# When the accumulators of a finished pass are emptied: at once, or one entry later

## The chip, the cores and the metric

The kernel runs on one core of one Trainium2 chip. The metric is the time of one execution on the device in microseconds (us), as the median of several runs. The chip's engines work beside each other, each through its own queue in order: TensorE (PE in the profile) multiplies matrices and sums into PSUM, VectorE (DVE) and ScalarE (ACT) do elementwise work, GpSimd (POOL) and SyncE (SP) do little here beyond starting DMA transfers.

## The reference

One layer of a hybrid decoder trunk over 512 tokens of width 2048, in float32:

```python
h = _rms_norm(x, norm_g[i])
proj = jnp.einsum("bld,dn->bln", h, w_in[i])
(z_ssd, xbc, dt, u_pool, z_pool, q, k, v, z_attn, gate_logits) = jnp.split(proj, IN_SPLITS, axis=-1)
...
gates = jax.nn.sigmoid(gate_logits.reshape(b, seq, N_BRANCHES, D_MODEL))
```

Three branches (a state-space scan, a causal pooling, a dilated attention) follow, are weighted by `gates`, summed and projected. What matters here is a part of `proj`: the columns for q, k, v and z_attn (five blocks of 1024 columns) and those for the gates (six blocks of 1024 columns).

## The kernel before

Each float32 operand is split in two parts, `hi` and `lo`, and a product is three matmuls: hi with hi, hi with lo, lo with hi. For weights that are streamed in, `split` does this: ScalarE casts to `hi` (L153), VectorE subtracts to get `lo` (L156). Both have three buffers, so a cast must wait until the entry three before has been multiplied. Between the two, L155 lets VectorE make the operand sum of the entry behind it (`mix`) if there is one. `split(idx + 2)` runs two entries ahead of the one that is multiplied.

The eleven blocks are computed by `s_block` with seven products in place of eight, in the manner of Strassen and Winograd: sums of the weight quarters a, b, c, d (T1, T2, T3, T4) are multiplied with sums of the quarters of h (S1 to S4, made once) or with the quarters themselves (L11, L12, L22). A block has three passes over four steps `e` of the contraction: L11, S2, S3 in the first, S4 and S1 in the second, L12 and L22 in the third; L12 goes on in L11's accumulators. One product at one step is an *entry*: 12 matmuls of 128x128 by 128x512 (L364), four steps each, 28 entries a block. Each product has two accumulators of one PSUM bank each, for the two halves of its rows, called `pg`; in this phase there are six such banks (`set_banks(2)`).

When a product is complete (e is 3), `after` empties its accumulators: L11 is copied by ScalarE (L330), the others are added by VectorE into `st` tiles in SBUF (L332, L335, L337, L340, L341, L347). At the end of S1 and of L22 two results of 512 columns each are complete, and L12 gives another; `evac` sends them out: in the gate blocks ScalarE takes a sigmoid (L566) and starts the store (L568) on its own DMA queue, in the q/k/v blocks it copies where needed (L574) and starts the store (L576). The order of work on each engine is the order in which the program is written; nothing is rescheduled. SP loads the weights, issued by `load` inside `split`.

So on VectorE and ScalarE there stand, entry by entry, the split for two entries ahead, and at the end of a pass the emptying of the accumulators, which needs TensorE to be done with that entry.

Of the kernel before, what the change touches and what calls it, by code (L numbers as in the profile page):

```python
# [31 lines left out]
def hybrid_kernel(ctx: ExitStack, tc: tile.TileContext, x, p, norm_g, w_in, conv_w, conv_b, dt_bias, a_log,  # L32
# [17 lines left out]
    def swap(name, as_=None):  # L50
        held["stack"].close()
        held["stack"] = ctx.enter_context(ExitStack())
        if name == "tp":
            held["tp"] = held["stack"].enter_context(tc.tile_pool(name="tq", bufs=NT))
        else:
            held["sp"] = held["stack"].enter_context(tc.tile_pool(name="sp", bufs=1))
# [9 lines left out]
    def set_banks(n):  # L66

        if banks:
            banks["stack"].close()
        banks["n"] = n  # L70
        banks["stack"] = ctx.enter_context(ExitStack())
        banks["psum"] = banks["stack"].enter_context(tc.tile_pool(name=f"psum{len(plan)}", bufs=3, space=PSUM))
# [4 lines left out]
    def PG():  # L77
        return banks["psum"].tile([128, L], F32, name="pg", tag="g", bufs=8 - banks["n"])
# [18 lines left out]
    def tick():  # L97
        now["t"] += 1
        step(other)
        step(tasks)  # L100
        step(third)
# [30 lines left out]
    def split(n):  # L132
        while state["split"] <= n and state["split"] < len(plan):
            i = state["split"]
            if callable(plan[i]) and "sp" not in held:
                return
            load(i)
            if callable(plan[i]):
                plan[i]("mix")
                r, k, c = plan[i]("raw"), 2, L  # L140
            else:
                r = raws.pop(i)
                _, k, c = plan[i]
            if c == 32:

                hl = wp.tile([128, k, 2 * c], F32R, name="hi", tag="hi")
                A.copy(hl[:, :, 0:c], r)
                V.tensor_sub(hl[:, :, c:], r, hl[:, :, 0:c].bitcast(F32))
                parts[i] = hl
            else:  # L150
                hi = wp.tile([128, k, c], F32R, name="hi", tag="hi")
                lo = wp.tile([128, k, c], F32R, name="lo", tag="lo")
                A.copy(hi, r)  # L153
                if state["dma"] > i + 1 and callable(plan[i + 1]):
                    plan[i + 1]("mix")  # L155
                V.tensor_tensor(lo, r, hi.bitcast(F32), op=ALU.subtract)  # L156
                parts[i] = (hi, lo)
            if callable(plan[i]):
                plan[i]("done")
            state["split"] += 1  # L160
            load(i + 3)
# [63 lines left out]
    def hook(f):  # L225
        jobs.append((f, lambda: None))
# [10 lines left out]
    def left(name, kt, t):  # L237
        c = slice(128 * t, 128 * t + 128)
        if name[0] == "L":
            q = slice(256 * (name[1] == "2") + 128 * t, 256 * (name[1] == "2") + 128 * t + 128)  # L240
            kt += 8 * (name[2] == "2")
            return HT[0][:, kt, q], HT[1][:, kt, q]
        return SC[name][0][:, kt, c], SC[name][1][:, kt, c]

    def make_left():
# [8 lines left out]
        for q0 in (0, 4):  # L254
# [13 lines left out]
            for n, o in (("S2", "L11"), ("S3", "S3"), ("S4", "L12"), ("S1", "L22")):  # L268
# [3 lines left out]
                if n in ("S3", "S1"):  # L272
                    yield

    def s_block(c0, evac):
        raw, ps, st = {}, {}, {}

        def src(n, e):
            r = e * 256 + (1024 if n in "cd" else 0)
            c = c0 + (L if n in "bd" else 0)  # L280
            return w_in[r:r + 256, c:c + L].rearrange("(k p) c -> p k c", p=128)

        def fetch(n, e, small):
            if small:
                t = held["sp"].tile([128, 2, L], F32, name="rs", tag="rs", bufs=2)
            else:
                t = wp.tile([128, 2, L], F32, name="raw", tag="raw", bufs=3)
            nc.sync.dma_start(out=t, in_=src(n, e))
            raw[n, e] = t

        def entry(name, e, loads):
            mixed = []

            def f(what):
                if what == "load":
                    for n, small in loads:
                        fetch(n, e, small)
                elif what == "mix":
                    if mixed:
                        return  # L300
                    mixed.append(1)
                    if name == "T2":
                        V.tensor_sub(raw["b", e], raw["d", e], raw["b", e])
                        t = held["sp"].tile([128, 2, L], F32, name="t2", tag="t2", bufs=4)
                        V.tensor_add(t, raw["b", e], raw["a", e])
                        raw["T2", e] = t
                    elif name == "T1":
                        t = held["sp"].tile([128, 2, L], F32, name="t1", tag="rs", bufs=2)
                        V.tensor_sub(t, raw["d", e], raw["T2", e])
                        raw["T1", e] = t  # L310
                    elif name == "T4":
                        V.tensor_sub(raw["T2", e], raw["T2", e], raw["c", e])
                elif what == "raw":
                    return raw[{"T3": "b", "T4": "T2"}.get(name, name), e]
            plan.append(f)
            return len(plan) - 1

        passes = []
        passes.append([(entry("a", e, (("a", False),)), entry("T2", e, (("b", True), ("d", False))),
                        entry("T3", e, ())) for e in range(4)])  # L320
        passes.append([(entry("d", e, (("d", False),)), entry("T1", e, ())) for e in range(4)])
        passes.append([(entry("c", e, (("c", False),)), entry("T4", e, ())) for e in range(4)])
        lefts = (("L11", "S2", "S3"), ("S4", "S1"), ("L12", "L22"))

        def after(name):
            for t in range(2):
                p = ps[name][t]
                if name == "L11":
                    st["u2", t] = st_tile()
                    A.copy(st["u2", t], p)  # L330
                elif name == "S2":
                    V.tensor_add(st["u2", t], st["u2", t], p)  # L332
                elif name == "S3":
                    st["u3", t] = st_tile()
                    V.tensor_add(st["u3", t], st["u2", t], p)  # L335
                elif name == "S4":
                    V.tensor_add(st["u2", t], st["u2", t], p)  # L337
                elif name == "S1":
                    o = st_tile()
                    V.tensor_add(st["u2", t], st["u2", t], p)  # L340
                    V.tensor_add(o, st["u3", t], p)  # L341
                    evac(t, 1, st["u2", t], st["u2", t])
                    evac(2 + t, 1, o, o)
                elif name == "L12":
                    evac(t, 0, p, st_tile())
                elif name == "L22":
                    V.tensor_sub(st["u3", t], st["u3", t], p)  # L347
                    evac(2 + t, 0, st["u3", t], st["u3", t])

        def run():  # L350
            for es, names in zip(passes, lefts):
                for e in range(4):
                    for idx, name in zip(es[e], names):
                        split(idx + 2)
                        hi, lo = parts.pop(idx)
                        if e == 0:
                            ps[name] = ps.pop("L11") if name == "L12" else [PG(), PG()]
                        for t in range(2):
                            for k in range(2):
                                kt = 2 * e + k  # L360
                                xh, xl = left(name, kt, t)
                                first, last = e == 0 and k == 0 and name != "L12", e == 3 and k == 1
                                for i, (lh, r) in enumerate(((xh, hi), (xh, lo), (xl, hi))):
                                    PE.matmul(ps[name][t], lhsT=lh, rhs=r[:, k], start=first and i == 0,  # L364
                                              stop=last and i == 2, skip_group_check=name in ("L11", "L12"))
                        if e == 3:
                            after(name)
                        tick()
        jobs.append((None, run))


# [59 lines left out]
    def st_tile():  # L431
        return held["sp"].tile([128, L], F32, name="st", tag="st", bufs=8)
# [195 lines left out]
    for br in (2, 0, 1):  # L628
        for j in (0, 2):
            s_block(GATES + br * D + j * L, gate_evac(br, j))  # L630
    hook(lambda: (swap("tp"), set_banks(3)))


    qT, kT, vv, oo, stat = {}, {}, {}, {}, {}
# [744 lines left out]
```

## Time and profile before

| | us |
|---|---|
| median of 3 runs | 2635.47 |
| lowest, highest | 2631.3, 2638.95 |
| the profiled execution | 2636.33 |
| its span, first to last instruction | 2634.5 |
| TensorE busy | 2594.7 (98%) |
| VectorE busy | 1545.5 (59%) |
| ScalarE busy | 1004.3 (38%) |

The seven-product phase runs from 151 to about 1009 us of the span, the five q/k/v blocks first (to 588 us), then the six gate blocks. A matmul's row shows its start and a modelled length; matmuls overlap, so lost time is read from the distance of two starts. "Granted clock" is the share of TensorE's full clock: 1.00 or 0.50.

### The profile page before, as it was taken

Reading aid. Unit: us, or ns where it says so; the run is one execution under the profiler, and the core shown is the slowest. Engines: PE = TensorE matmul, PEld = TensorE weight load, DVE = VectorE, ACT = ScalarE, POOL = GpSimd, SP = SyncE. Lnnn points to the kernel's source line nnn. Section 1 sums busy time; section 2 is a strip of 40 time slices with the busy share of each in tenths; the row PEclk is TensorE's granted clock in tenths of the full one; section 3 lists DMA queues with packets and bytes.
Section 4 is the critical chain, followed back from the end, with each engine's and each line's share of the span. In section 5 each row is a group of like instructions: output and inputs, shape, how many; then the busy total and the mean of one; then the engine's idle time right before and its main releaser. Section 6 shows DMA issues by size and latency. Waiting matters only on the chain.

```text
span 2634.5 us, 30399 instructions
## 1 busy us (share of the span) xinstructions
PE 2594.7 (98%) x11924; PEld 2136.4 (81%) x11924; DVE 1545.5 (59%) x1926; ACT 1004.3 (38%) x1275; POOL 190.9 (7%) x213
## 2 busy tenths in 40 slices
PE   9999999999999999999999999999999999999998
PEld 7778888887778787888888888877888888788887
DVE  5767777777777774454536567786642433233333
ACT  5434444444444443343434544543321322232322
POOL 2000000000000000101010001231011111000000
PEclk9999999999999999999999999999999999999999
DMA  6445555455554454434343444463543633333442
GB/s 226 117 136 176 176 164 160 149 160 168 171 173 145 148 155 139 125 104 144 113 140 120 132 125 139 124 186 113 153 147 113 211 107 125 104 121 112 130 142 96
DMA packets 237647, 374.52 MB, mean 142 GB/s; under 512 B 17208, under 2 KB 102020, under 8 KB 236992
## 3 DMA queue, kind: packets, MB, share of 16 engines
q1 hardware_dynamic: 218384, 331.31, 42.0%
q10 hardware_dynamic: 13904, 25.30, 2.6%
q0 software_dynamic: 5216, 15.98, 1.6%
q8 instruction: 93, 1.52, 0.2%
q14 instruction: 50, 0.41, 0.0%
HBM read 330.30 MB, written 42.23 MB: 141 GB/s over the span
## 4 chain that ended last, share of the span: by engine, by line
PE 90%; DVE 4%; ACT 3%; issue 1%; ACTq 1%; DMA 1%; POOL 0%; SPq 0%; DVEq 0%
PE pg L364 28%; PE pg L166 19%; PE pg L167 19%; PE pg L168 19%; ACT hi L153 1%; DVE lo L156 1%; ACT st L566 1%; PE ps L518 1%; PE ps L1079 1%; ACTq L568 1%; PE ps L797 0%; PE ps L761 0%; PE ps L1062 0%; DVE bc L1032 0%; PE ps L716 0%
## 5 line engine op out<-in xcount | busy, mean ns | idle before, releaser
L156 DVE TENSOR_TENSOR lo<-raw,hi 128x1024 fp32r<-128x1024 f32 x424 | 523.0, 1234 | 636.8 <-ACT hi L153 635.0
L153 ACT CAST hi<-raw 128x1024 fp32r<-128x1024 f32 x424 | 444.7, 1051 | 792.3 <-PE pg L168 440.1
L166 PE MATMUL pg<-hh,hi 128*128 128x512 f32 x1152 | 460.7, 400 | 2.0 <-ACT st L566 2.0
L168 PE MATMUL pg<-hh,lo 128*128 128x512 f32 x1152 | 449.6, 390 | 0.0
L167 PE MATMUL pg<-hl,hi 128*128 128x512 f32 x1152 | 449.2, 390 | 0.0
L166 PEld LDWEIGHTS pg<-hh,hi 128*128 128x128 f32 x1152 | 216.8, 188 | 49.9 <-issue 3.3
L168 PEld LDWEIGHTS pg<-hh,lo 128*128 128x128 f32 x1152 | 216.5, 188 | 46.0
L167 PEld LDWEIGHTS pg<-hl,hi 128*128 128x128 f32 x1152 | 216.8, 188 | 45.2 <-issue 2.4
L156 DVE TENSOR_TENSOR lo<-t,hi 128x1024 fp32r<-128x1024 f32 x132 | 161.6, 1224 | 105.8 <-ACT hi L153 105.3
L153 ACT CAST hi<-t 128x1024 fp32r<-128x1024 f32 x132 | 138.8, 1052 | 204.5 <-PE pg L364 168.1
L364 PE MATMUL pg<-lo,hh 128*128 128x512 f32 x528 | 208.3, 394 | 7.0 <-DVE lo L156 7.0
L364 PE MATMUL pg<-hi,hh 128*128 128x512 f32 x528 | 208.0, 394 | 7.0 <-DVE st L612 4.8
L364 PE MATMUL pg<-hi,hl 128*128 128x512 f32 x528 | 206.8, 392 | 0.0
L364 PEld LDWEIGHTS pg<-lo,hh 128*128 128x128 f32 x528 | 100.1, 190 | 32.1 <-DVE lo L156 11.0
L364 PEld LDWEIGHTS pg<-hi,hh 128*128 128x128 f32 x528 | 99.9, 189 | 30.8 <-issue 5.2
L364 PEld LDWEIGHTS pg<-hi,hl 128*128 128x128 f32 x528 | 100.1, 190 | 20.6
L166 PE MATMUL pg<-hi,mh 128*128 128x512 f32 x256 | 100.7, 393 | 0.0
L166 PE MATMUL pg<-hi,yph 128*128 128x512 f32 x256 | 100.1, 391 | 0.0
L168 PE MATMUL pg<-hi,ml 128*128 128x512 f32 x256 | 99.9, 390 | 0.0
L167 PE MATMUL pg<-lo,mh 128*128 128x512 f32 x256 | 99.8, 390 | 0.0
L166 PE MATMUL pg<-hi,xh 128*128 128x512 f32 x256 | 99.8, 390 | 0.0
L168 PE MATMUL pg<-hi,ypl 128*128 128x512 f32 x256 | 99.7, 389 | 0.0
(355 smaller groups left out, 4546.1 us busy)
## 6 DMA issues: line engine op xcount, KB each, us to landing
raw<-in_w_in_dram SPq DMA_DIRECT2D x320, 512.0 KB, 3.8
rs<-in_w_in_dram SPq DMA_DIRECT2D x44, 512.0 KB, 4.6
raw<-in_w_br_ssd_dram SPq DMA_DIRECT2D x32, 512.0 KB, 3.8
raw<-in_w_br_pool_dram SPq DMA_DIRECT2D x32, 512.0 KB, 3.9
raw<-in_w_out_dram SPq DMA_DIRECT2D x32, 512.0 KB, 3.7
raw<-in_w_ple_gate_dram SPq DMA_DIRECT2D x32, 512.0 KB, 3.7
gate_d<-st ACTq DMA_DIRECT2D x48, 256.0 KB, 2.3
g<-gate_d SPq DMA_DIRECT2D x48, 256.0 KB, 5.2
```

Source lines behind the costliest of these rows:

```text
L153: A.copy(hi, r)
L156: V.tensor_tensor(lo, r, hi.bitcast(F32), op=ALU.subtract)
L166: PE.matmul(ps, lhsT=lh, rhs=rh, start=first, stop=False)
L167: PE.matmul(ps, lhsT=lh, rhs=rl, start=False, stop=False)
L168: PE.matmul(ps, lhsT=ll, rhs=rh, start=False, stop=last)
L364: PE.matmul(ps[name][t], lhsT=lh, rhs=r[:, k], start=first and i == 0, stop=last and i == 2, skip_group_check=name in ("L11", "L12"))
L518: PE.matmul(ps[:, o:o + 128], lhsT=xt[2 * f + t][:, rows(2 * j + k)], rhs=diag[f][:, rows(t)], start=True, stop=True)
L566: A.activation(o, src, AF.Sigmoid)
L568: nc.scalar.dma_start(out=gate_d[br, rows(t), c:c + L], in_=o)
L1079: PE.matmul(pd[q, rows(h // 2)], lhsT=xdt[:, h * 64:h * 64 + 64], rhs=bc[h // 4][:, rows(h % 4)], start=True, stop=True)
```

## The change

The call of `after` moves. An entry that ends a pass no longer empties its accumulators behind its own matmuls; it puts the call on a list, and the next entry carries it out behind its own `split` and ahead of its matmuls and of the allocation of its accumulators. The last entry of a block is emptied in the first entry of the next block, the last of all in the hook that closes the phase. The diff:

```diff
+    late = []
+
+    def evict_late():
+
+        while late:
+            late.pop(0)()
 
     def s_block(c0, evac):
...
                         split(idx + 2)
                         hi, lo = parts.pop(idx)
+                        evict_late()
                         if e == 0:
                             ps[name] = ps.pop("L11") if name == "L12" else [PG(), PG()]
...
                         if e == 3:
-                            after(name)
+                            late.append(lambda name=name: after(name))
                         tick()
...
-    hook(lambda: (swap("tp"), set_banks(3)))
+    hook(lambda: (evict_late(), swap("tp"), set_banks(3)))
```

## Rows read from the trace of the kernel before

**Rows 1.** The page: the chain that ended last, by line.
```profile
PE pg L364 28%; PE pg L166 19%; PE pg L167 19%; PE pg L168 19%; ACT hi L153 1%; DVE lo L156 1%; ACT st L566 1%; PE ps L518 1%; PE ps L1079 1%; ACTq L568 1%; PE ps L797 0%; PE ps L761 0%; PE ps L1062 0%; DVE bc L1032 0%; PE ps L716 0%
```

**Rows 2.** Busy time by stretches: stretch, length, engines' busy time, granted clock, DMA.
```profile
311.00:588.00 277.00, 277.00 (x1224) 229.03 (x1223) 216.04 (x204) 115.15 (x117) 0.00 (x0) 1.00 0.53 160
```

**Rows 3.** Waits, 588 to 1012 us: total us, times, longest.
```profile
PEld pg L364 <- DVE lo L156: 13.2, 16, 1.1
```

**Rows 4.** TensorE's timeline, first pass to second: start, length; first matmuls of entries.
```profile
643.23 0.39 PE L364 MATMUL pg<-hi,S3h 128*128 128x512 f32 x1
...
645.95 0.39 PE L364 MATMUL pg<-hi,S4h 128*128 128x512 f32 x1
...
648.67 0.39 PE L364 MATMUL pg<-hi,S1h 128*128 128x512 f32 x1
```

**Rows 5.** TensorE's timeline, behind a second pass (gate block).
```profile
594.08 0.39 PE L364 MATMUL pg<-hi,hl 128*128 128x512 f32 x1
594.68 0.49 PE L364 MATMUL pg<-hi,hh 128*128 128x512 f32 x1 [0.21 <-ACT hi L153]
595.94 0.50 PE L364 MATMUL pg<-lo,hh 128*128 128x512 f32 x1 [0.77 <-DVE lo L156]
596.28 0.39 PE L364 MATMUL pg<-hi,hl 128*128 128x512 f32 x1
```

**Rows 6.** TensorE's timeline, start of the next block (gate).
```profile
617.61 0.39 PE L364 MATMUL pg<-hi,S3h 128*128 128x512 f32 x1
...
620.64 0.39 PE L364 MATMUL pg<-hi,hh 128*128 128x512 f32 x1
621.55 0.50 PE L364 MATMUL pg<-lo,hh 128*128 128x512 f32 x1 [0.52 <-DVE lo L156]
```

**Rows 7.** ScalarE's timeline, 585 to 666 us.
```profile
589.33 0.63 ACT L566 ACTIVATE st<-st 128x512 f32<-128x512 f32 x1 [0.59 <-DVE st L340]
...
593.58 1.05 ACT L153 CAST hi<-raw 128x1024 fp32r<-128x1024 f32 x1 [0.45 <-ACT st L566]
...
615.66 1.05 ACT L153 CAST hi<-rs 128x1024 fp32r<-128x1024 f32 x1 [0.40 <-ACT st L566]
...
643.48 1.05 ACT L153 CAST hi<-t 128x1024 fp32r<-128x1024 f32 x1 [1.23 <-PE pg L364]
```

**Rows 8.** VectorE's timeline, first pass to second (and one single add, 588.62).
```profile
588.62 0.68 DVE L340 TENSOR_TENSOR st<-st,pg 128x512 f32<-128x512 f32 x1
...
645.75 1.27 DVE L335 TENSOR_TENSOR st<-st,pg 128x512 f32<-128x512 f32 x2
646.95 1.22 DVE L309 TENSOR_TENSOR t<-raw,t 128x1024 f32<-128x1024 f32 x1
648.09 1.22 DVE L156 TENSOR_TENSOR lo<-raw,hi 128x1024 fp32r<-128x1024 f32 x1
```

**Rows 9.** VectorE's timeline, second-pass end and block start (gate).
```profile
587.48 1.22 DVE L156 TENSOR_TENSOR lo<-t,hi 128x1024 fp32r<-128x1024 f32 x1 [0.30 <-ACT hi L153]
...
617.88 1.22 DVE L303 TENSOR_TENSOR rs<-raw,rs 128x1024 f32<-128x1024 f32 x1
...
620.28 1.22 DVE L156 TENSOR_TENSOR lo<-raw,hi 128x1024 fp32r<-128x1024 f32 x1
```

**Rows 10.** ScalarE's timeline, second-pass end of a q/k/v block.
```profile
281.65 1.05 ACT L153 CAST hi<-t 128x1024 fp32r<-128x1024 f32 x1 [1.67 <-PE pg L364]
...
286.83 1.05 ACT L153 CAST hi<-raw 128x1024 fp32r<-128x1024 f32 x1 [4.12 <-DVE st L341]
```

**Rows 11.** Busy time by stretches, first and last gate block (columns as in rows 2).
```profile
592.85:596.25 3.40, 2.42 (x10) 1.48 (x9) 1.59 (x2) 2.95 (x4) 0.00 (x0) 1.00 0.41 154
988.80:992.20 3.40, 1.82 (x7) 1.16 (x7) 2.45 (x3) 2.82 (x3) 0.00 (x0) 1.00 0.25 83
992.20:995.60 3.40, 3.40 (x10) 2.61 (x9) 2.18 (x2) 0.36 (x1) 0.00 (x0) 0.50 0.56 157
1008.00:1013.00 5.00, 2.98 (x13) 2.17 (x12) 2.42 (x3) 2.26 (x4) 0.00 (x0) 1.00 0.81 251
```

## The prediction

> **What bounds the kernel now.** I read the page first: the chain that ended last runs through TensorE's matmuls, those of the seven-product phase (L364) first with 28% of the span [rows 1]. So a change there counts only as far as it moves matmul starts. Next I took the busy time by stretches: in the q/k/v blocks TensorE is busy for all of the 277.00 us between 311 and 588 us [rows 2]. Nothing can be gained there; a new wait can only cost. Then the waits of TensorE in the six gate blocks: its weight loads waited 16 times for the subtraction `lo` [rows 3]. The timeline shows that these are two places that repeat: the end of the second pass (six times) and the start of the next block (five times, two waits each).
>
> An entry is 12 matmuls and takes 2.72 us (645.95 to 648.67 [rows 4]), 0.227 us a matmul. At the end of the second pass the starts lie 0.60, 1.26 and 0.34 us apart [rows 5]: 0.37 + 1.03 + 0.11 = 1.5 us lost, the last term being what a restart costs. At a block's start S3 began at 617.61, the next entry at 620.64 instead of 620.33, and its second matmul 0.91 later [rows 6]: 0.31 + 0.68 + 0.11 = 1.1 us lost. All of it, 6 x 1.5 + 5 x 1.1 = 14.5 us, is what waits can give back; the one fall of the clock behind such a wait (below) comes on top.
>
> Why those waits: ScalarE's first S1 sigmoid starts at 589.33, the cast queued behind the four sigmoids and their stores at 593.58 [rows 7], 4.25 us later, and that cast's entry was due at 594.08 + 0.23 = 594.31 us [rows 5], before the cast could end at 594.63.
>
> **The change part by part.** No instruction is added or removed. In an entry that ends a pass the adds, copies, sigmoids and their stores on ScalarE's DMA queue move behind the next entry's cast and subtraction, and behind the operand sum (`mix`) that L155 puts between these two. SP's loads stand in no order with them. The moved work is late by the length of what it is moved past; who waits for it then is the question. There are five places.
>
> *First pass to second, all 11 blocks.* S4 and S1 need four accumulator banks, and all six are taken: L11's pair lives on, so S4 must get S2's pair and S1 gets S3's. Today S4 starts at 645.95 and S1 at 648.67 without a gap [rows 4], and the adds for S3 run from 645.75 to 646.95 [rows 8], S2's before them. After the change S2's adds stand behind the split of the second T1 operand. Its cast starts at 643.48 [rows 7], 0.25 after S3 starts, when its buffer comes free, and cannot be earlier; the subtraction follows when the cast is done, 1.08 later at 644.56, and the add 1.14 behind that (the spacing from a subtraction at 587.48 to an add at 588.62 [rows 8, 9]), at 645.70. One add takes 0.68 [rows 8], so the first bank is free at about 646.43: S4 starts 0.48 late, and 0.11 goes into the restart. The pair occupies VectorE for 1.20 (645.75 to 646.95 [rows 8]), then come `mix` L309 and the subtraction of the next d, 1.14 each: S3's first add runs from 649.18 to 649.86, the bank is free at 649.91. S1 is due at 648.67 + 0.59 = 649.26: 0.65 + 0.11 lost. The second bank is needed 1.36 later and is free in time. Sum 1.35 us a block, 11 x 1.35 = +14.8 us. The trace of before does not show this wait: below it is bounded by nothing (if the banks are other ones), above by a wait for both adds, 0.60 more each, 2 x 0.6 x 11 = 13 us more. I take the first bank alone, since each bank has its own matmuls.
>
> *Second pass to third, six gate blocks.* S1's adds start at 588.62 today, right behind the subtraction for T4's first entry at 587.48 [rows 8, 9]; that subtraction ends a wait for its cast, so it stays where it is. Now S4's pair (1.20), `mix` L312 (1.14) and the next c's subtraction (1.14) stand between: 3.48 us later, at 592.10. The cast queued behind the sigmoids is now that of one entry later, due 2.72 us later. So it starts at 593.58 + 3.48 = 597.06 and is 3.48 - 2.72 = 0.76 us later against its due time than today's. The wait isn't taken away but grows from 1.5 to 2.3 us: 6 x 0.76 = +4.6 us.
>
> *The same place in the five q/k/v blocks.* The cast behind the stores starts at 286.83 [rows 10]; 3.48 later is 290.31. Its entry is due at 281.40 + 2.72 + 8.16 = 292.28 (281.40 is the start of S1, 0.25 before the cast at 281.65 [rows 10]), so the cast is in time, but the subtraction (1.08 after it, 1.23 long) ends at 292.62 and is due at 292.51: 0.1 to 0.15 and a restart, 5 x 0.25 = +1.3 us; bounds 0 and 5 x 0.76.
>
> *Third pass to the next block, five gate boundaries.* Here the order helps. Today the cast of T3 starts at 615.66 behind L22's sigmoids [rows 7], and the subtraction for the next a at 620.28 behind both operand sums at 617.88 [rows 9]. In the new order the cast for T2 starts with its buffer at 609.70 (the entry due at 617.61 - 3 x 2.72 = 609.45, and 0.25) and L12's two sigmoids with their stores follow it, 1.06 each (4.25 / 4), until 612.9. T3's cast, whose buffer is free at 612.4, starts then. Its subtraction ends at 615.2, L22's first add at 615.8, the pair at 616.3, the two sums (2.40, 617.88 to 620.28) at 618.7, and the cast of a, behind L22's two sigmoids, at 618.95. So the next a's subtraction ends at 620.2 and is due at 617.61 + 2.72 + 0.23 = 620.56. Both waits go: 5 x 1.1 = -5.5 us. S3 at 617.61 finds L22's banks free since 616.3.
>
> *The end of the phase.* The next stage's first matmul waits for the last block's evictions: 2.98 of 5.00 us are busy [rows 11]. One cast now precedes L12's sigmoids instead of following them, so L22's adds come about 1.0 earlier: -1.0 us, bounds 0 and -2.0.
>
> Sum without the clock: 14.8 + 4.6 + 1.3 - 5.5 - 1.0 = +14.2 us.
>
> *The clock.* Around the last of the second-pass waits TensorE was busy for 1.82 of 3.40 us; the granted clock of the next 3.40 us was 0.50, the lower of its two levels (1.2 instead of 2.4 GHz), and half of that time, 1.7 us, was lost [rows 11]. At the first gate block's wait of 1.5 us TensorE was busy for 2.42 of 3.40 us and the clock stayed at 1.00 [rows 11], as it did at the four others between these two; and it stayed at 1.00 when TensorE stood idle for 2.0 us at the end of the phase (1008 to 1013 us [rows 11]). The new 2.3 us are nearest to these last cases, one with a fall and one without, so I count half of six places: three falls for today's one, +3.4 us; bounds -1.7 (none) and +8.5 (all six). The Trainium skill, "TensorE: Matmul & The Clock Gate", section "A second HAM failure mode: psum-queue depth-cycling", says that a kernel which cycles through PSUM banks leaves TensorE idle for moments between groups, often enough for the clock to swing between its two levels; by it the bank waits themselves would pull the clock down too. The trace disagrees for waits as short as these: 1.5 us left the clock at 1.00.
>
> In all +17.6 us. The profiled execution took 2636.33 us (0.9 above the median of the three runs, 2635.47): 2636.3 + 17.6 = 2654 us.
>
> **The rivals.**
> 1. *The bank waits are hidden*, because S4 and S1 get banks that have long been emptied. For it: no wait of TensorE for a bank stands in the trace. Against it: six banks, three pairs in use. Without the 14.8 us: 2639 us, no change that can be told (this kernel's runs tell about 0.3%, 7.9 us). Chance 0.09.
> 2. *Faster: the split ahead of the eviction frees the second-pass end too.* This is so if VectorE reaches the moved adds earlier than I count: S1's adds 1.13 us earlier (its sigmoids done by 595.93 instead of 597.06) and S2's 0.48 earlier. VectorE idles between subtractions in the trace, which speaks for it; against it, the idle spells end with a cast [rows 9], and the cast waits for TensorE to free its buffer [rows 7]. Then 9.0 + 5.5 + 1.0 + 1.7 (no fall) are saved: 2619 us. Chance 0.06.
> 3. *The clock falls behind the bank waits as well*, 11 places, and at all six gate places: 14.2 + 16 x 1.7 = +41.4, 2678 us. Against it the waits of 1.5 us without a fall. Chance 0.04. This is what the page named above would make of the bank waits.
>
> **How the numbers follow.** My forecast has 0.81; within it the clock alone moves the time from 2649 (no fall) to 2659 us (six), and the bounds of the q/k/v term and of the bank wait add some on either side. The range 2642 to 2665 leaves out rivals 1 to 3 and a little of the forecast. Slower by over 0.3%: 0.81 + 0.04 = 0.85; within 0.3%: 0.09; faster: 0.06.
>
> **What would show it.** In the changed kernel's profile: TensorE waits for the adds at L332 and L335 (now behind the split) in all 11 blocks, about 0.5 and 0.65 us; TensorE no longer busy for all of a q/k/v block; the wait at the second pass's end one entry later and near 2.3 us; no wait at the start of a gate block; two to four stretches with the clock at 0.50 in the gate blocks. I am wrong if no matmul waits at the first S4 or S1 entry, or if the second-pass wait is gone.

## The result, and the profile after

| | before | after |
|---|---|---|
| median | 2634.12 us (4 runs) | 2655.76 us (4 runs) |
| span of the profiled execution | 2634.5 us | 2652.5 us |
| the seven-product phase, its first matmul to the next stage's first | 859.9 us | 877.9 us |

The change made the kernel slower: ratio 1.0078, 95% interval 1.0066 to 1.009. 2654 us had been forecast. Of the 18.0 us by which the span grew, 17.9 lie in the seven-product phase (877.85 - 859.91), so the rest of the kernel can be left aside. The medians lie 21.6 us apart. What follows accounts for the 18.0 us between one profiled execution of each kernel. Executions of one kernel differ with the clock: of 27 of the kernel before on one chip, the 11 with a mean granted clock of 0.995 took 2637.2 us in the mean, the 8 with 0.997 took 2633.7.

Seven lines were added ahead of `s_block`, so line numbers are higher: the matmul is L372, the adds for S2, S3, S4, S1 are L339, L342, L344, L347 and L348, the operand sums L309 and L312 are L316 and L319, the gate's sigmoid is L574 (L577 in runs with three more lines), the q/k/v store L584.

First the end of the first pass, in the first gate block. TensorE's timeline around S4's and S1's first matmuls, which answers to [rows 4]:

```profile
658.19 0.39 PE L372 MATMUL pg<-hi,S3l 128*128 128x512 f32 x1
659.00 0.47 PE L372 MATMUL pg<-hi,S4h 128*128 128x512 f32 x1 [0.42 <-DVE st L339]
659.31 0.39 PE L372 MATMUL pg<-lo,S4h 128*128 128x512 f32 x1
...
661.61 0.39 PE L372 MATMUL pg<-hi,S4l 128*128 128x512 f32 x1
662.47 0.47 PE L372 MATMUL pg<-hi,S1h 128*128 128x512 f32 x1 [0.46 <-DVE st L342]
```

Two starts that belong 0.227 us apart lie 0.81 and 0.86 apart, and the releasers are the adds that free S2's and S3's banks. S4's first matmul does not wait for the pair, only for the first add (658.17 + 0.68 = 658.85). VectorE's timeline of the same stretch shows why, beside [rows 8]:

```profile
657.03 1.23 DVE L156 TENSOR_TENSOR lo<-t,hi 128x1024 fp32r<-128x1024 f32 x1 [1.54 <-ACT hi L153]
658.17 1.28 DVE L339 TENSOR_TENSOR st<-st,pg 128x512 f32<-128x512 f32 x2
659.37 1.22 DVE L316 TENSOR_TENSOR t<-raw,t 128x1024 f32<-128x1024 f32 x1
660.50 1.22 DVE L156 TENSOR_TENSOR lo<-raw,hi 128x1024 fp32r<-128x1024 f32 x1
661.64 1.28 DVE L342 TENSOR_TENSOR st<-st,pg 128x512 f32<-128x512 f32 x2
```

S2's pair now comes behind the subtraction that a cast holds up, and S3's behind another operand sum and another subtraction. The spacings are those of before: 1.14, 1.20, 1.13, 1.14.

The end of the second pass, TensorE's timeline in the first gate block, beside [rows 5]:

```profile
609.72 0.39 PE L372 MATMUL pg<-hi,hl 128*128 128x512 f32 x1
611.01 0.50 PE L372 MATMUL pg<-hi,hh 128*128 128x512 f32 x1 [0.90 <-ACT hi L153]
612.27 0.50 PE L372 MATMUL pg<-lo,hh 128*128 128x512 f32 x1 [0.76 <-DVE lo L156]
612.61 0.39 PE L372 MATMUL pg<-hi,hl 128*128 128x512 f32 x1
```

The first distance was 0.60 and is 1.29; the second and third are the same. The start of the next block, beside [rows 6]:

```profile
631.22 0.39 PE L372 MATMUL pg<-hi,S3h 128*128 128x512 f32 x1
...
633.94 0.39 PE L372 MATMUL pg<-hi,hh 128*128 128x512 f32 x1
634.17 0.39 PE L372 MATMUL pg<-lo,hh 128*128 128x512 f32 x1
```

2.72 us for the entry and 0.23 to the second matmul: this wait is gone. Last, busy time by stretches (columns as in [rows 2, 11]), first the q/k/v blocks, where TensorE had no idle time before, then stretches of the gate blocks:

```profile
311.00:588.00 277.00, 272.19 (x1189) 221.99 (x1188) 209.97 (x198) 111.02 (x114) 0.00 (x0) 1.00 0.54 161
...
853.10:856.50 3.40, 1.76 (x6) 1.23 (x7) 2.54 (x3) 1.86 (x3) 0.00 (x0) 1.00 0.79 302
856.60:860.00 3.40, 3.40 (x17) 2.81 (x16) 3.36 (x4) 1.91 (x2) 0.00 (x0) 1.00 0.39 96
...
689.40:692.80 3.40, 1.75 (x7) 0.92 (x6) 1.97 (x2) 1.99 (x2) 0.00 (x0) 1.00 0.97 358
692.90:696.30 3.40, 3.40 (x9) 2.64 (x8) 3.37 (x4) 1.05 (x1) 0.00 (x0) 0.50 0.26 32
```

The clock fell behind two of the six second-pass waits (the one before 692.9 and one before 774.8), for before's one. The two waits shown left TensorE equally busy, 1.76 and 1.75 us; one was followed by the full clock, the other by half.

For the whole phase I added up, for each kernel's profiled execution, the distances between neighbouring starts over 0.227 us (where the excess is over 0.04), and sorted them by entry. "Behind the second pass" is the wait of T4's second entry in the new order, of c's second in the old; for the gate blocks it contains what the lower clock right behind it cost, and the last column but one counts those falls. Left out are 1.5 to 2.3 us at the phase's first matmuls, which every kernel here starts at a granted clock of 0.50, and at most 0.5 us in a kernel elsewhere.

| lost us in the phase | at S4, S1 (11 blocks) | behind 2nd pass, q/k/v | behind 2nd pass, gates | start of block | end of phase | clock falls there | phase |
|---|---|---|---|---|---|---|---|
| before | 0 | 0 | 11.6 | 5.3 | 2.2 | 1 | 859.9 |
| after | 15.5 | 3.4 | 16.7 | 0 | 1.1 | 2 | 877.9 |
| late_8banks | 0 | 3.1 | 15.1 | 0 | 1.1 | 1 | 859.8 |
| late_first | 15.2 | 0 | 9.8 | 5.8 | 2.2 | 0 | 874.5 |
| late_s3_only | 7.2 | 0 | 11.7 | 5.3 | 2.2 | 1 | 868.1 |
| late_second | 0 | 3.1 | 19.9 | 5.3 | 2.2 | 4 | 871.6 |
| late_s1_only | 0 | 0 | 9.1 | 5.4 | 2.2 | 0 | 856.7 |
| late_third | 0 | 0 | 9.7 | 0 | 1.1 | 0 | 851.2 |
| late_qkv_pool | 15.3 | 0 | 19.7 | 0 | 1.1 | 4 | 876.2 |
| stores_late | 0 | 0 | 0.9 | 0.2 | 1.1 | 0 | 841.7 |
| now_8banks | 0 | 0 | 9.4 | 5.3 | 2.2 | 0 | 858.2 |

### The profile page after: what moved, and what is told of

The parts are those of the page before. It is cut to its first block, busy times and chain, and to the rows that moved or that the text cites. A ratio compares the mean times of both kernels' runs of the same rounds, so it can differ in the third digit from the quotient of the medians.

```text
span 2652.5 us, 30367 instructions
## 1 busy us (share of the span) xinstructions
PE 2600.4 (98%) x11924; PEld 2137.3 (81%) x11924; DVE 1547.1 (58%) x1926; ACT 1003.8 (38%) x1275; POOL 190.3 (7%) x213
## 4 chain that ended last, share of the span: by engine, by line
PE 86%; DVE 7%; ACT 3%; issue 2%; DMA 1%; ACTq 0%; SPq 0%; POOL 0%; DVEq 0%
PE pg L372 25%; PE pg L166 19%; PE pg L168 19%; PE pg L167 19%; DVE lo L156 2%; ACT hi L153 2%; ACT st L574 1%; PE ps L1087 1%; DVE st L344 0%; DVE st L339 0%; PE ps L526 0%; PE ps L805 0%; DMA x<-in_x_dram 0%; PE ps L769 0%; DVE st L347 0%
## 5 line engine op out<-in xcount | busy, mean ns | idle before, releaser
L372 PE MATMUL pg<-hi,hh 128*128 128x512 f32 x528 | 208.5, 395 | 10.5 <-ACT hi L153 5.7
L372 PE MATMUL pg<-lo,hh 128*128 128x512 f32 x528 | 208.9, 396 | 6.6 <-DVE lo L156 6.6
L372 PE MATMUL pg<-hi,hl 128*128 128x512 f32 x528 | 207.8, 393 | 0.0
L372 PEld LDWEIGHTS pg<-hi,hh 128*128 128x128 f32 x528 | 100.5, 190 | 34.4 <-ACT hi L153 8.2
L372 PEld LDWEIGHTS pg<-lo,hh 128*128 128x128 f32 x528 | 100.4, 190 | 31.4 <-DVE lo L156 10.6
L372 PEld LDWEIGHTS pg<-hi,hl 128*128 128x128 f32 x528 | 100.4, 190 | 20.8
```

## The experiments

The theory: the loss is made of the bank waits at S4 and S1, a longer wait behind the second pass and falls of the clock behind that; only the third pass gains. The main rival: the moved splits themselves come late, whatever the banks. Ratios are to the kernel before on the same chip.

**Banks.** The changed kernel with two more accumulator banks, so that S4's first pair is free from the start:

```diff
-    hook(lambda: (flush(), set_banks(2)))
+    hook(lambda: (flush(), set_banks(0)))
```

> The changed kernel with eight accumulator banks in the phase where it had six (nothing else uses the two others there). Theory (S4 and S1 wait for banks whose adds now stand behind the split): the two waits at the end of the first pass go in all 11 blocks, 11 x 1.37 = 15.1 us, so 2655.8 - 15.1 = 2641 us; the q/k/v blocks then lose only what stands behind the second pass. Rival (the loss is the reordered queues themselves, splits that come late, not banks): within 3 us of the changed kernel, 2653 to 2656 us.

Measured: 2634.83 us, ratio 0.9997 (0.9988 to 1.0006). TensorE's timeline at the same place (first gate block) has no gap left:

```profile
650.65 0.39 PE L372 MATMUL pg<-hi,S3l 128*128 128x512 f32 x1
650.87 0.39 PE L372 MATMUL pg<-hi,S4h 128*128 128x512 f32 x1
...
653.59 0.39 PE L372 MATMUL pg<-hi,S1h 128*128 128x512 f32 x1
```

The rival falls: the order of the queues is the changed kernel's, and the waits at S4 and S1 are gone. The time is 6 us below what was expected. Of the 20.4 us between the two spans (2652.5 and 2632.1), 15.5 are the bank waits, 1.6 the gate blocks' waits with one fall of the clock less, 2.4 lie outside the phase, and the rest is small differences. The control, the same edit in the kernel before:

> The kernel before with eight accumulator banks in the phase. Theory (before, no matmul waits for a bank): no change, within 3 us of the kernel before. Rival (banks are short before the change as well): several us faster.

Measured: 2633.65 us, ratio 0.9993 (0.9984 to 1.0002). Banks were not short before; the change made them so.

**One pass late at a time.** Each of these replaces the new line by a choice; the others are emptied at once.

```diff
-                            late.append(lambda name=name: after(name))
+                            if name in ('L11', 'S2', 'S3'):
+                                late.append(lambda name=name: after(name))
+                            else:
+                                after(name)
```

> Only L11, S2 and S3 are emptied one entry late. Theory: two bank waits in each of 11 blocks, 15 us, 2634.1 + 15 = 2649 us. Rival (the waits need the other two passes' delays as well): 2634 to 2640 us.

Measured: 2650.85 us, ratio 1.0054 (1.0041 to 1.0066). The first pass alone costs the 15 us.

With `("S3",)` in that place:

> Only S3 is emptied one entry late. Theory: S2's banks are free when S4 starts (no wait); S3's first add stands behind the operand sum L309 and the subtraction of the next d, ends 0.5 us after S1 is due, and with the restart 0.5 to 0.6 us are lost in each of 11 blocks: 6 us above the kernel before. Rival (the wait comes only when both products are late): no change.

Measured: 2642.33 us, ratio 1.0027 (1.0018 to 1.0036); S4 does not wait, S1 waits 11 times, 7.2 us in all. So S1's wait needs S3's late add alone. S2's late add alone was not run; in late_first, with both, S4 waits 7.2 us and S1 8.0.

With `('S4', 'S1')`:

> Only S4 and S1 are emptied one entry late. Theory: the moved adds come 3.48 us later and the cast behind them is due only 2.72 us later, so the wait of the gate blocks grows by 0.7 to 0.8 us each (4 to 5 us) and the q/k/v blocks get one of 0.5 to 0.8 us each (3 us), with one or two falls of the clock more: 2641 to 2645 us. Rival (the split ahead of the eviction frees the second-pass end): 2625 us.

Measured: 2650.38 us, ratio 1.005 (1.0037 to 1.0062). The direction is the theory's, the size is not: the gate blocks' waits were as expected (2.2 us each), but the clock fell behind four of the six, and three falls more than before make about 5 us.

With `('S1',)`:

> Only S1 is emptied one entry late; S4 and all others at once. Theory (the wait behind the second pass is a balance of the length of what the adds are moved past against one entry of 2.72 us): without S4's pair the adds come 1.14 + 1.14 = 2.28 us later, 0.44 less than the entry, so the gate wait shrinks from 1.5 to about 1.1 us and the q/k/v blocks wait for nothing: about 2.6 us below the kernel before, 2632 to 2634 us beside a kernel before at 2635 to 2636. Rival (any lateness of S1's adds makes the wait longer): 4 to 8 us above the kernel before.

Measured: 2635.8 us, ratio 0.9998 (0.9989 to 1.0007): neither the theory's time nor the rival's. VectorE's timeline of this kernel, first gate block:

```profile
588.81 1.22 DVE L319 TENSOR_TENSOR t<-t,raw 128x1024 f32<-128x1024 f32 x1
590.39 1.23 DVE L156 TENSOR_TENSOR lo<-raw,hi 128x1024 fp32r<-128x1024 f32 x1 [0.36 <-ACT hi L153]
591.53 0.68 DVE L347 TENSOR_TENSOR st<-st,pg 128x512 f32<-128x512 f32 x1
```

My 2.28 us left out that the subtraction has to wait for its cast, and the cast for its buffer, which comes free once per entry. The adds start 1.14 behind a subtraction held by a cast, as they did before, one entry of 2.72 us later; so does the cast that is due one entry later, and the wait stays at 1.5 us (9.1 / 6). Behind a split an eviction is late by an entry at least, and by more when other work fills the queue, as S4's pair does in the change.

With `('L12', 'L22')`:

> Only L12 and L22 are emptied one entry late; the other products at once, as before. Theory (the third pass is the one place where the order helps): 5 x 1.1 at the block starts and about 1.0 at the end of the phase, 2634.1 - 6.5 = 2628 us, with no wait at a block's start and the second-pass waits of 1.5 us as before. Rival (what is saved at the block start is waited for later in the first pass): 2634 us.

Measured: 2626.75 us, ratio 0.9965 (0.9953 to 0.9978). The gain at the block starts is real, 5.3 us, and is not given back. Of the 8.7 us by which the phase is shorter than before's, 1.1 more are its end and 1.9 the gate waits, here without a fall of the clock.

**The stores of the q/k/v blocks.** The wait of 3.4 us there was more than twice what I had counted. TensorE's timeline in the second q/k/v block of the changed kernel, then one store's issue there (the third of four), then one of before:

```profile
296.63 0.39 PE L372 MATMUL pg<-hi,hh 128*128 128x512 f32 x1
297.46 0.50 PE L372 MATMUL pg<-lo,hh 128*128 128x512 f32 x1 [0.44 <-DVE lo L156]
...
293.60 0.67 ACTq L584 DMA_DIRECT2D qkv_d<-st  x1
...
284.59 0.33 ACTq L576 DMA_DIRECT2D qkv_d<-st  x1
```

The changed kernel with these stores started by GpSimd:

```diff
-            nc.scalar.dma_start(out=qkv_d[rows(t), c:c + L], in_=o)
+            G.dma_start(out=qkv_d[rows(t), c:c + L], in_=o)
```

> The changed kernel, but the stores of the q/k/v blocks are started by GpSimd instead of ScalarE. Theory (in the changed kernel the q/k/v blocks wait behind the second pass because the four stores hold ScalarE's queue, two of them 0.67 instead of 0.33 us, ahead of the cast): the cast starts with its buffer, the 3.4 us of those waits go, and the time is 2652 to 2653 us. Rival (the wait comes from VectorE's queue, the subtraction standing behind S1's adds): no change, 2656 us.

Measured: 2655.9 us, ratio 1.0075 (1.0062 to 1.0089). First ScalarE's timeline in the changed kernel, then in this one:

```profile
288.72 1.05 ACT L153 CAST hi<-raw 128x1024 fp32r<-128x1024 f32 x1 [1.67 <-PE pg L372]
292.40 2.60 ACTq L584 DMA_DIRECT2D qkv_d<-st  x4
295.10 1.05 ACT L153 CAST hi<-t 128x1024 fp32r<-128x1024 f32 x1 [5.33 <-DVE st L348]
```

```profile
286.93 1.06 ACT L153 CAST hi<-raw 128x1024 fp32r<-128x1024 f32 x1 [1.67 <-PE pg L372]
289.65 1.06 ACT L153 CAST hi<-t 128x1024 fp32r<-128x1024 f32 x1 [1.66 <-PE pg L372]
```

There the cast started 6.38 us after the one before it, here 2.72, and the waits of the q/k/v blocks are gone (3.4 to 0). So the stores in ScalarE's queue made these waits, as the theory has it. The whole time did not fall with it, against the theory: in the profiled execution the clock fell behind four gate waits for two, about 3 us. The other executions point the same way: the mean granted clock of all five is 0.993 to 0.994, that of the changed kernel's four 0.993 to 0.995. Why the clock fell more often, and whether it takes back all of the 3.4 us, stays open.

**A version that keeps the gain.** S1's adds at once, its sigmoids and stores behind the next split, L12 and L22 late, the rest at once:

```diff
-                    evac(t, 1, st["u2", t], st["u2", t])
-                    evac(2 + t, 1, o, o)
+                    late.append(lambda t=t, o=o: (evac(t, 1, st["u2", t], st["u2", t]),
+                                                  evac(2 + t, 1, o, o)))
...
-                            late.append(lambda name=name: after(name))
+                            if name in ('L12', 'L22'):
+                                late.append(lambda name=name: after(name))
+                            else:
+                                after(name)
```

> S1's adds on VectorE are done at once, as before; its sigmoids and stores on ScalarE come behind the next split; L12 and L22 are emptied one entry late; L11, S2, S3 and S4 at once. Theory: no add is moved past a subtraction that a wait hangs on, the cast behind the second pass starts with its buffer and the sigmoids end 2 us before the next cast's entry is due, so the 11 us behind the second pass, the 5.3 us at the block starts and about 1 us at the phase's end all go: 17 us below the kernel before, 2617 to 2619 us. Rival (the sigmoids, later by an entry, make the next cast late): at most the 6.5 us of the third pass, 2628 to 2630 us.

Measured: 2618.74 us, ratio 0.9935 (0.9922 to 0.9947): faster than both kernels. ScalarE's timeline, second-pass end of the first gate block:

```profile
589.05 1.05 ACT L153 CAST hi<-raw 128x1024 fp32r<-128x1024 f32 x1 [1.67 <-PE pg L372]
590.12 1.28 ACT L577 ACT_TABLE_LOAD   x1
591.41 0.63 ACT L577 ACTIVATE st<-st 128x512 f32<-128x512 f32 x1
...
595.66 1.05 ACT L153 CAST hi<-t 128x1024 fp32r<-128x1024 f32 x1 [0.45 <-ACT st L577]
```

The cast at 589.05 starts with its buffer, ahead of the sigmoids, which wait for no add. In this block alone the table load (1.28) holds them up, and the next cast with them: of the 11.6 us behind the second pass 0.9 are left. Against late_third, which differs only in that S1's sigmoids and stores stand where they stood, the gates' waits go from 9.7 to 0.9 us. In the q/k/v and gate blocks together 841.7 us are used for matmuls that need 838.3 (3696 starts by 0.2268). No fall of the clock is left there, and the five executions lie within 0.8 us.

## Why the prediction was right

- **First pass to second.** Forecast +14.8, found +15.5: 1.41 us a block for 1.35. The waits, their releasers and the rule that the first bank alone counts are as forecast; six banks make it (late_8banks), and S3's moved add alone makes S1's half (late_s3_only).
- **Second pass to third, gates.** Forecast 0.76 us more a block; the first distance grew by 0.69. Without the clock the six waits grew by 3.5 us (13.5 for 10.0) where 4.6 were forecast. The prediction took all six of before's waits for 1.5 us; four were, the third was 1.8 and the last, the one with the fall behind it, 2.1. late_s1_only shows that the sum left out a floor, and that it came out right all the same is luck: 3.48 us holds because S4's pair fills the queue past the cast; without it the answer is 2.72, not 2.28.
- **The same in the q/k/v blocks.** This term was mis-sized: forecast +1.3, found +3.4. I took the stores' issue times from before. In the change two of a block's four issues took about 0.7 us instead of 0.33 (the four 2.60 us in all), and the cast behind them came 0.4 us later than worked out (9.35 us behind the start of S1's last entry, for 8.91); over five blocks that is about the 2.1 us missing. late_qkv_pool shows that these stores make the wait; what their longer issue adds was not tested by itself.
- **Start of the next block** -5.5 forecast, -5.3 found; **end of the phase** -1.0 and -1.1.
- **The clock.** Three falls were forecast for one, two came: about +1.6 for +3.4. This made up for the q/k/v term. Over the four kernels with the waits of 2.2 us (after, late_8banks, late_second, late_qkv_pool) the clock fell behind 11 of 24, so counting half was fair, but a single kernel had one to four. What decides is open, so that two came and not four is luck. Behind the bank waits, 77 of 0.7 to 0.9 us in four kernels (22 each in after, late_first and late_qkv_pool, 11 in late_s3_only), it never fell. What the prediction drew from the Trainium skill, "TensorE: Matmul & The Clock Gate", section "A second HAM failure mode: psum-queue depth-cycling", a lower clock behind the bank waits, did not come.
- **Rivals.** The hidden bank waits fell with the first timeline, the faster case with that of the second pass's end, where the wait is longer and not gone. What the faster case looked for does exist, but only when the adds stay where they were and the sigmoids alone move (stores_late).

Sum: 15.5 + 3.4 - 5.3 - 1.1 + 5.1 (16.7 - 11.6 in the gates, falls included) = 17.6 us, of 17.9 in the phase. That this is the forecast's +17.6 to the tenth is luck: the first pass and the q/k/v blocks came 2.8 us dearer than forecast, the gate blocks with their clock 2.9 us cheaper.

## What to carry to other kernels

Before moving an eviction behind other work, count the banks that are free at the next allocation: where the next product takes the very bank, TensorE waits for as long as the first add ends after that product is due. A cast that waits for a buffer sets the pace of the queue behind it, so "behind the next split" meant one entry later at least here, and nothing is won if what it was blocking is also due one entry later. What paid here was to part the eviction: the step that frees the bank stays early, the step that only sends the result out goes behind what TensorE waits for.

## What the runs showed of the hardware that was not expected

- A store's issue on ScalarE's queue took 0.32 to 0.33 us in all 40 q/k/v stores of before, and up to 0.78 after the change; from issue to landing their median was 2.3 us before and 5.2 after. In the changed kernel two loads of SyncE (291.80 and 292.22 us) go out just ahead of the stores (292.40); before, the same two went out behind them (the second at 289.59, stores from 284.59). The same holds in every kernel whose q/k/v stores are ScalarE's: in the four that empty S1 late (after, late_8banks, late_second, late_s1_only) the first of the two loads goes out 0.6 us ahead in all 20 places, and the longer of the third and fourth issue there took 0.47 to 0.87 us; in the six others the two loads come over 4 us behind the first store, and in 29 of 30 places all four issues took 0.33 us. In stores_late the landing takes 2.6 us. That the loads are the cause is argued from this order, not shown.
- The gates' second-pass waits of 2.2 to 2.5 us in after, late_8banks, late_second and late_qkv_pool were followed by the full clock or by half of it (11 of 24 by half), two of them with the same busy time around them. Three of 2.1 to 2.2 us in other kernels (before, late_s3_only, late_first) were followed by half, half and full. Behind the 33 waits of 1.5 to 1.8 us in the kernels that empty S4 at once the clock never fell. What decides among the longer ones is open.
